# A dilated-attention layer with gated MLP: five step times of the attention plan moved, so that its small matmuls stand in other places

## The chip, the cores and the metric

One core of one Trainium2 chip. The metric is device microseconds (us) of one execution; the kernel before takes 1303.2 us, the median of three runs (1301.95 to 1303.62). Engines are named as the profile names them: PE is TensorE (PEld its weight loads), DVE is VectorE, ACT is ScalarE, POOL is GpSimd, SP is the queue that issues the DMAs.

## What is computed

One layer of a decoder trunk on 1024 tokens of width 1024. The mixer is a dilated sliding-window attention with 3 groups (dilations 1, 4, 16) of 8 heads of 64; the groups are merged by their softmax denominators. After it comes a gated MLP of 2 x 2816 channels with a short causal convolution. Cut to what matters:

```
h = rms_norm(x, mixer_norm)
proj = (h @ w_in).reshape(B, S, 3 groups, 3, 8 heads, 64)
for g, (window, dilation) in enumerate(((128, 1), (512, 4), (2048, 16))):
    q = rms_norm(proj[:, :, g, 0], q_gain[g]) * 64 ** -0.5
    k = rms_norm(proj[:, :, g, 1], k_gain[g])
    o, lse = dilated_window_attention(q, k, proj[:, :, g, 2], window, dilation)
o = sum over groups of softmax(lse) * o
x = x + o @ w_out
x = x + conv_ffn(rms_norm(x, ffn_norm))
```

All is in float32. A product of two float32 matrices is made of three matmuls on numbers split into a high and a low part.

## The kernel before

The attention runs as 48 blocks: 6 units (a group and half of its heads: group 2, then 1, then 0, two units each) of 8 blocks of 128 tokens. Units are counted from 0 here, blocks from 0 to 47; units 4 and 5 are the last group, and their blocks also merge the three groups. Of a block, PE makes the projection of q and k (lines 207 to 209, matmuls of 512 columns, 24 of them), the projection of v (lines 216 to 218, 256 columns, 24 of them) and small work: four transposes of the normed q and k (line 265, tile `tr`), the scores (lines 294, 298), the transposes of the softmax weights of heads 0 and 1, then of heads 2 and 3 (line 331, tile `pt`), and the second products, weights times v, for the same two pairs of heads (lines 349 and 351, tile `u`, 128 and 64 columns). A block with a previous block of keys (22 of the 48) has twice the weights: 4 transposes and 8 second products for a pair of heads, the others 2 and 4.

Nothing is scheduled by a planner. Every step of a block is put into one list with a time, counted in steps of one projection slice; a block has 8. The list is sorted by time, equal times in the order in which they were added, and PE, ACT, DVE and POOL each run their instructions in just that order. For block i:

```
e = 8 * i + 8
at(8 * i + k, b.project, k)                      # k = 0..7
at(8 * i + T["vs"] * k + T["v"], b.project_v, k) # 2.6 + 0.85 k
at(e + T[name] + late, step, *args)              # all other steps
```

So a block's small steps lie between the projections of the two blocks after it. The steps in question, by their name in the table `T` (line 35):

- `w0`, `w1` (weights_T): the transposes of the weights on PE. `ws0`, `ws1` (weights_split): each result is copied to its high part by ACT (line 337) and the low part is made by DVE (line 338, tile `pT`).
- `a0`, `a1` (attend): the second products on PE. A first matmul of a pair needs the high part, the second (line 351) the low part.
- `scale` (line 229, DVE, tile `qn`): the normed q and k of the next block. `hT` (line 265, PE) transposes them, `hs` splits them on ACT and DVE (lines 276 to 282), and the scores follow. `scale` needs the reciprocal root `rs` from POOL (line 80).
- `mw` (units 4 and 5): line 370 and 372 on DVE, line 373 (an exponential) on ACT, line 375 and on on POOL.
- `load_w`: the split of the next unit's projection weights, the high part on ACT (line 188), the low part on DVE or POOL (line 189).
- Behind the last blocks the second phase begins: line 628 and 629 split the output weights, lines 584 to 586 are the output projection, line 588 adds it to x, and `norm2` (line 593 on ACT, line 595 on DVE) norms the sum.

Times of other steps that lie near: `scale` of the next block at e + 10.5, its `hT` at e + 12.2, `mw` at e + 10.0, `load_w` at e + 8.7, 9.45 and 10.6 (start of units 2 and 4) or e + 8.7, 9.6 and 10.8 (units 1, 3 and 5), `norm2` of the first output rows at e + 9.8 of block 47.

Of the kernel before, what the change touches and what calls it, by code (L numbers as in the profile page):

```python
# [32 lines left out]


T = dict(v=2.6, vs=0.85, w=3.1, norm=-0.2, val=0.6, kept=3.2, scale=2.5, hT=4.2, hs=4.45, sc=6.45,
         sm=6.5, w0=8.3, ws0=9.35, w1=10.0, ws1=11.95, mw=10.0, a0=12.2, a1=13.3, mo=12.2,
         fin=14.4, t0=4, so0=3.2, so1=3.3, so2=5.1, so3=5.2, to0=-3.43, to=-3.6, n2=3.0, n2s=5.8,
         xf=-9.8, xs=-5.0, xt=-3.5, wp=1, bd=0.5, bh=0)

# [1067 lines left out]
```

## Time and profile before

| | |
|---|---|
| median of 3 runs | 1303.2 us (1301.95 to 1303.62) |
| the profiled execution | 1301.99 us |
| its span, first to last instruction | 1300.0 us |
| PE busy | 1274.2 us, 98% of the span |
| DVE, ACT, POOL busy | 69%, 47%, 37% |
| granted clock of PE | 0.999 |

The attention's blocks fill the span from about 11 to 582 us, some 11.9 us each; the output projection and the MLP follow. A timeline row gives an instruction's start from the span's start, its duration, engine, line, output and inputs, and in brackets the idle time of its engine before it and who ended that. Rows of matmuls overlap: PE takes the next one before the last has drained. So what a matmul costs is read from start to start, not from its duration.

### The profile page before, as it was taken

The numbers are of one execution on the slowest core, as the hardware profiler recorded it, in microseconds if no ns is written. First come the engines' busy times: TensorE is split into PE (matmuls) and PEld (weight loads), VectorE is DVE, ScalarE is ACT, GpSimd is POOL, SyncE is SP. The second block draws the span as 40 slices with busy tenths as digits, with TensorE's granted clock in tenths as the row PEclk, the third lists the DMA queues.
The fourth block names the chain that finished last, engine by engine and source line by source line (L and its number), as shares of the span: only waits on it lengthen the run. The fifth ranks groups of instructions, "written<-read, shape, count | busy, mean of one in ns | idle before, by whom it ended". The sixth has DMA issues, their size and how long they took to land.

```text
span 1300.0 us, 19219 instructions
## 1 busy us (share of the span) xinstructions
PE 1274.2 (98%) x6911; PEld 1071.0 (82%) x6911; DVE 896.2 (69%) x1542; ACT 617.1 (47%) x1284; POOL 486.7 (37%) x596
## 2 busy tenths in 40 slices
PE   7999999999999999999998999999999999999998
PEld 6888888888888888887886788888888887888887
DVE  5665555555555665557876988888888888876664
ACT  5555454444464454345644454544544545444441
POOL 4333443332454555535523544444444442000000
PEclk9999999999999999999999999999999999999999
DMA  7112112111131221023711333233233229963341
GB/s 263 38 54 79 38 38 60 47 48 52 46 109 51 62 63 37 27 70 132 235 35 43 120 122 122 81 114 105 66 122 122 81 81 326 367 212 97 97 143 63
DMA packets 111614, 132.16 MB, mean 102 GB/s; under 512 B 6126, under 2 KB 80030, under 8 KB 111518
## 3 DMA queue, kind: packets, MB, share of 16 engines
q1 hardware_dynamic: 111518, 130.93, 31.5%
q8 instruction: 55, 0.90, 0.3%
q14 instruction: 41, 0.34, 0.1%
HBM read 95.91 MB, written 35.00 MB: 101 GB/s over the span
## 4 chain that ended last, share of the span: by engine, by line
PE 43%; DVE 4%; ACT 2%; issue 1%; DMA 1%; POOL 0%; SPq 0%; DVEq 0%; POOLq 0%; ACTq 0%
PE y L902 15%; PE ua L718 15%; PE uc L718 8%; PE ub L718 4%; DVE c L763 2%; ACT c L761 1%; DMA x<-in_x 1%; DMA graw<-gde 0%; DVE bt L629 0%; DVE sz L691 0%; DVE c L774 0%; DVE xn L595 0%; DMA wB<-in_ffn_w_down 0%; DVE sy L687 0%; POOL b L629 0%
## 5 line engine op out<-in xcount | busy, mean ns | idle before, releaser
L902 PE MATMUL y<-wd,g 128*128 128x512 f32 x924 | 210.4, 389 | 0.2
L902 PEld LDWEIGHTS y<-wd,g 128*128 128x128 f32 x924 | 173.4, 188 | 36.9 <-DVE wd L629 0.6
L207 PE MATMUL qk<-w,hh 128*128 128x512 f32 x384 | 157.5, 410 | 0.1
L208 PE MATMUL qk<-w,hh 128*128 128x512 f32 x384 | 152.8, 398 | 0.3 <-DVE w L189 0.3
L209 PE MATMUL qk<-w,hl 128*128 128x512 f32 x320 | 126.1, 394 | 0.0
L79 POOL TENSOR_SCALAR ms<-ss 128x8 f32<-128x8 f32 (+1 forms) x64 | 12.8, 201 | 296.6 <-DVE ss L225 254.0
L763 DVE SCALAR_TENSOR_TENSOR c<-uu,cw,c 128x1023 f32<-128x1023 f32 (+1 forms) x44 | 97.0, 2205 | 37.1 <-ACT c L761 36.3
L216 PE MATMUL vp<-w,hh 128*128 128x256 f32 x384 | 122.0, 318 | 0.4 <-DVE v L237 0.2
L217 PE MATMUL vp<-w,hh 128*128 128x256 f32 x384 | 107.9, 281 | 0.0
L549 POOL TENSOR_TENSOR wyl<-sy,wyh 128x1024 fp32r<-128x1024 f32 x21 | 56.9, 2708 | 109.3 <-issue 55.3
L80 POOL TENSOR_TENSOR rs<-ms,half 128x8 f32<-128x8 f32 (+1 forms) x64 | 89.0, 1391 | 5.3
L218 PE MATMUL vp<-w,hl 128*128 128x256 f32 x320 | 90.0, 281 | 0.0
L323 ACT ACTIVATE sm<-sm,ust 128x128 f32<-128x128 f32 (+1 forms) x128 | 53.3, 418 | 77.0 <-DVE ust L320 74.5
L216 PEld LDWEIGHTS vp<-w,hh 128*128 128x128 f32 x384 | 72.8, 189 | 15.2 <-DVE v L237 2.4
L225 DVE TENSOR_REDUCE ss<-qn 128x8 f32<-128x512 f32 x48 | 32.9, 685 | 75.6 <-ACT qn L223 75.6
L276 ACT ACTIVATE qT<-tr,gains 128x256 fp32r<-128x256 f32 x48 | 22.7, 474 | 122.0 <-PE tr L265 122.0
L217 PEld LDWEIGHTS vp<-w,hh 128*128 128x128 f32 x384 | 72.8, 190 | 9.1
L279 DVE SCALAR_TENSOR_TENSOR qT<-tr,gains,qT 128x256 fp32r<-128x256 f32 x48 | 23.1, 482 | 81.4 <-ACT kT L278 81.4
L208 PEld LDWEIGHTS qk<-w,hh 128*128 128x128 f32 x384 | 73.1, 190 | 1.5 <-DVE w L189 1.0
L207 PEld LDWEIGHTS qk<-w,hh 128*128 128x128 f32 x384 | 73.0, 190 | 0.7 <-ACT hh L116 0.5
L320 DVE CUSTOM_DVE_ANT_0 sm<-s,mask 128x128 f32<-128x128 f32 (+1 forms) x192 | 56.0, 347 | 24.0 <-PE s L298 18.5
L209 PEld LDWEIGHTS qk<-w,hl 128*128 128x128 f32 x320 | 60.5, 189 | 14.6 <-DVE hl L117 0.2
(193 smaller groups left out, 3395.7 us busy)
## 6 DMA issues: line engine op xcount, KB each, us to landing
uraw<-in_ffn_w_up SPq DMA_DIRECT2D x44, 512.0 KB
raw<-in_attn_w_in SPq DMA_DIRECT2D x48, 384.0 KB
wB<-in_ffn_w_down SPq DMA_DIRECT2D x44, 256.0 KB
graw<-gds SPq DMA_DIRECT2D x44, 256.0 KB
gdo<-c SPq DMA_DIRECT2D x11, 512.0 KB
gds<-gbc SPq DMA_DIRECT2D x11, 512.0 KB
graw<-gdo SPq DMA_DIRECT2D x22, 256.0 KB
ud<-ust SPq DMA_DIRECT2D x32, 132.0 KB
```

Of the source, the lines that this page charges most:

```text
L80: nc.gpsimd.tensor_tensor(r[:, :n], t[:, :n], half[:, :n], op=ALU.pow)
L207: nc.tensor.matmul(self.qk, a, w[:, 0, :512], start=k == 0, stop=False)
L208: nc.tensor.matmul(self.qk, a, w[:, 1, :512], start=False, stop=False)
L209: nc.tensor.matmul(self.qk, b, w[:, 0, :512], start=False, stop=k == KT - 1)
L216: nc.tensor.matmul(self.vp, a, w[:, 0, 512:], start=k == 0, stop=False)
L217: nc.tensor.matmul(self.vp, a, w[:, 1, 512:], start=False, stop=False)
L218: nc.tensor.matmul(self.vp, b, w[:, 0, 512:], start=False, stop=k == KT - 1)
L320: nc.vector.tensor_tensor_reduce(out=sm[:, h, lo:], in0=src[h], in1=m, op0=ALU.add, op1=ALU.min, scale=-1.0, scalar=3e38, accum_out=st[:, ...
L549: eng.tensor_sub(l, raw, h.bitcast(F32))
L718: nc.tensor.matmul(acc[:, lo:hi], w[z][:, s + k], a[y][:, j, k, lo:hi], start=begin and lo == 0 and k == 0 and n == 0, stop=k == 3 and n == 2,
L763: nc.vector.scalar_tensor_tensor(c[:, k:], u[:, :S - k], cw[:, 2 - k, j:j + 1], c[:, k:], op0=ALU.mult, op1=ALU.add)
L902: nc.tensor.matmul(y, gs[:, z, ts], ws[:, w], start=f and n == 0, stop=k == NK - 1 and n == 2, skip_group_check=True)
```

## The change

Five numbers of the table are changed: `w0` from 8.3 to 9.0, `ws0` from 9.35 to 9.9, `w1` from 10.0 to 9.05, `ws1` from 11.95 to 10.5, and `a1` from 13.3 to 12.25. Each holds for all 48 blocks. No instruction is added or dropped.

```diff
-         sm=6.5, w0=8.3, ws0=9.35, w1=10.0, ws1=11.95, mw=10.0, a0=12.2, a1=13.3, mo=12.2,
+         sm=6.5, w0=9.0, ws0=9.9, w1=9.05, ws1=10.5, mw=10.0, a0=12.2, a1=12.25, mo=12.2,
```

On PE, the transposes of the weights in a block without previous keys; `vp` and `qk` are the projections of later blocks. Before:

```order
2066 L331 MATMUL pt<-ident,sm 128x128 x2
2067 L216 MATMUL vp<-w,hh 128x256
2068 L217 MATMUL vp<-w,hh 128x256
2069 L218 MATMUL vp<-w,hl 128x256
2070 L207 MATMUL qk<-w,hh 128x512
2071 L208 MATMUL qk<-w,hh 128x512
2072 L209 MATMUL qk<-w,hl 128x512
2073 L331 MATMUL pt<-ident,sm 128x128 x2
```

The same place after:

```order
2066 L216 MATMUL vp<-w,hh 128x256
2067 L217 MATMUL vp<-w,hh 128x256
2068 L218 MATMUL vp<-w,hl 128x256
2069 L331 MATMUL pt<-ident,sm 128x128 x2
2070 L207 MATMUL qk<-w,hh 128x512
2071 L208 MATMUL qk<-w,hh 128x512
2072 L209 MATMUL qk<-w,hl 128x512
2073 L331 MATMUL pt<-ident,sm 128x128 x2
```

The first pair moves behind three matmuls of 256 columns; the second pair keeps its place, and a slice of the q and k projection (whose time, 9.0, equals the new `w0` and comes before 9.05) still stands between the two.

On PE, the second products in such a block; `tr` are the next block's transposes of q and k, behind `a0`:

```order
 L351 MATMUL u<-v,pT 128x64
 L265 MATMUL tr<-ident,qn 128x128 x4
+L349 MATMUL u<-v,pT 128x128
+L351 MATMUL u<-v,pT 128x64
+L349 MATMUL u<-v,pT 128x128
+L351 MATMUL u<-v,pT 128x64
 L216 MATMUL vp<-w,hh 128x256
 L217 MATMUL vp<-w,hh 128x256
```

The second products of heads 2 and 3 now follow `tr` at once; before they stood three slices of projection later.

On DVE, a block of units 4 and 5 with previous keys; `pT` is the low part of `ws1`, `qn` the next block's `scale`:

```order
 L370 TENSOR_REDUCE nm<-mt 128x4
 L372 TENSOR_TENSOR e<-nm,mt 128x12
-L229 TENSOR_TENSOR qn<-qk,rs 128x512
-L338 TENSOR_TENSOR pT<-pt,pT 128x512
+L338 TENSOR_TENSOR pT<-pt,pT 128x512
+L229 TENSOR_TENSOR qn<-qk,rs 128x512
 L386 RECIPROCAL rz<-z 128x4
 L279 SCALAR_TENSOR_TENSOR qT<-tr,gains,qT 128x256
```

`ws1` and `scale` change places, since both stand at 10.5 and the earlier block's step was added first. It is so in every block.

On DVE, block 47, where the second phase has begun; `x_7030` and `x_7033` are the same tile, the first output rows, in before and after. Before:

```order
893 L588 TENSOR_TENSOR x_7030<-x_7030,y 128x512
894 L338 TENSOR_TENSOR pT<-pt,pT 128x512
895 L595 SCALAR_TENSOR_TENSOR xn<-x_7030,rs,gbc 128x1024
896 L370 TENSOR_REDUCE nm<-mt 128x4
897 L372 TENSOR_TENSOR e<-nm,mt 128x12
898 L588 TENSOR_TENSOR x_7152<-x_7152,y 128x512
899 L338 TENSOR_TENSOR pT<-pt,pT 128x512
```

The same place after:

```order
859 L588 TENSOR_TENSOR x_7033<-x_7033,y 128x512
860 L595 SCALAR_TENSOR_TENSOR xn<-x_7033,rs,gbc 128x1024
861 L338 TENSOR_TENSOR pT<-pt,pT 128x512
862 L370 TENSOR_REDUCE nm<-mt 128x4
863 L372 TENSOR_TENSOR e<-nm,mt 128x12
864 L588 TENSOR_TENSOR x_7154<-x_7154,y 128x512
865 L338 TENSOR_TENSOR pT<-pt,pT 128x512
```

`ws0` of block 47 (9.9) moves behind `norm2` (9.8), here on DVE and in the same way on ACT. At the start of a unit `ws0` likewise moves behind one more `load_w` (9.45 or 9.6) on ACT and DVE, and `ws1` moves ahead of the one at 10.6 or 10.8.

## Rows read from the trace of the kernel before

**Rows 1.** The page's first part: busy time, share, instructions of PE.

```profile
PE 1274.2 (98%) x6911; PEld 1071.0 (82%) x6911; DVE 896.2 (69%) x1542; ACT 617.1 (47%) x1284; POOL 486.7 (37%) x596
```

**Rows 2.** Waits of PE and of DVE: who for whom, total us, times, longest us.

```profile
PE tr L265 <- DVE qn L229: 2.9, 5, 0.9
...
DVE qn L229 <- POOL rs L80: 42.0, 41, 1.5
```

**Rows 3.** Timeline of PE, `a1` of a block with previous keys, and behind it.

```profile
306.67 0.22 PE L349 MATMUL u<-v,pT 128*128 128x128 f32 x1
...
307.48 0.37 PE L216 MATMUL vp<-w,hh 128*128 128x256 f32 x1
307.68 0.29 PE L217 MATMUL vp<-w,hh 128*128 128x256 f32 x1
307.81 0.28 PE L218 MATMUL vp<-w,hx 128*128 128x256 f32 x1
```

**Rows 4.** Timeline of PE, `a1` of block 47, which stands between transposes.

```profile
604.66 0.31 PE L349 MATMUL u<-v,pT 128*128 128x128 f32 x1
...
605.55 0.33 PE L605 MATMUL xT<-ident,xn 128*128 128x128 f32 x1
```

**Rows 5.** Timeline, block 34 (unit 4): `mw`, `scale`, `ws1`, `tr`.

```profile
434.53 0.17 DVE L372 TENSOR_TENSOR e<-nm,mt 128x12 f32<-128x12 f32 x1
434.62 0.68 DVE L229 TENSOR_TENSOR qn<-qk,rs 128x512 f32<-128x512 f32 x1
...
435.45 0.69 DVE L338 TENSOR_TENSOR pT<-pt,pT 128x512 fp32r<-128x512 f32 x1 [0.15 <-ACT pT L337]
...
436.26 0.33 PE L265 MATMUL tr<-ident,qn 128*128 128x128 f32 x1
```

**Rows 6.** Timeline, block 43 (unit 5): `ws1` on ACT, `tr`.

```profile
545.95 0.57 ACT L337 CAST pT<-pt 128x512 fp32r<-128x512 f32 x1
...
548.42 0.33 PE L265 MATMUL tr<-ident,qn 128*128 128x128 f32 x1
```

**Rows 7.** Timeline, block 38, where unit 5's weights are split.

```profile
484.69 1.83 POOL L189 TENSOR_TENSOR w<-raw,w 128x768 fp32r<-128x768 f32 x1
...
484.82 1.72 DVE L372 TENSOR_TENSOR e<-nm,mt 128x12 f32<-128x12 f32 x1
...
486.47 0.68 DVE L229 TENSOR_TENSOR qn<-qk,rs 128x512 f32<-128x512 f32 x1
...
487.21 0.33 PE L265 MATMUL tr<-ident,qn 128*128 128x128 f32 x1 [0.49 <-DVE qn L229]
```

**Rows 8.** Timeline, block 30, where unit 4's weights are split.

```profile
387.38 0.68 DVE L229 TENSOR_TENSOR qn<-qk,rs 128x512 f32<-128x512 f32 x1
...
387.98 0.41 DVE L338 TENSOR_TENSOR pT<-pt,pT 128x256 fp32r<-128x256 f32 x1
...
388.11 0.33 PE L265 MATMUL tr<-ident,qn 128*128 128x128 f32 x1 [0.92 <-DVE qn L229]
```

**Rows 9.** Timeline, block 47: `ws0`, `norm2`, `a0`, `ws1`.

```profile
597.09 0.56 ACT L337 CAST pT<-pt 128x512 fp32r<-128x512 f32 x1
...
597.55 1.06 ACT L593 ACTIVATE xn<-x 128x1024 f32<-128x1024 f32 x1
...
599.65 1.29 DVE L595 SCALAR_TENSOR_TENSOR xn<-x,rs,gbc 128x1024 f32<-128x1024 f32 x1 [1.28 <-POOL rs L80]
...
600.26 0.22 PE L349 MATMUL u<-v,pT 128*128 128x128 f32 x1
...
601.97 0.69 DVE L338 TENSOR_TENSOR pT<-pt,pT 128x512 fp32r<-128x512 f32 x1 [0.16 <-ACT pT L337]
```

**Rows 10.** Timeline, `a1` of blocks 22 and 46: first matmuls.

```profile
294.24 0.22 PE L349 MATMUL u<-v,pT 128*128 128x128 f32 x1
...
294.55 0.30 PE L351 MATMUL u<-v,pT 128*128 128x64 f32 x1
...
589.50 0.30 PE L351 MATMUL u<-v,pT 128*128 128x64 f32 x1 [0.40 <-DVE pT L338]
```

## The prediction

> **What bounds the kernel now.** The page's first part comes first: PE is busy for 98% of the span [rows 1], so the end moves only with what PE itself costs or waits. Then the waits of PE and of DVE [rows 2]. In the attention PE waits above all for one thing, the transposes `tr` of the next block for DVE's `scale` (2.9 us in 5 waits), and DVE's `scale` itself mostly waits for POOL's `rs` (42.0 us in 41 waits). So DVE usually stands idle in front of `scale`, and whatever is put there is free as long as it fits; where it doesn't fit, PE waits at `tr`. Last the timeline, for two questions: what a group of small matmuls costs apart and joined [rows 3, 4], and how close each kind of block is to making `tr` wait [rows 5 to 9].
>
> **The joined groups on PE.** `a1` alone, 8 second products, runs from 306.67 to 307.48, 0.81 us, and the first big matmul behind it holds the next one off for 0.20 us where the one after takes 0.13 [rows 3]: 0.81 + 0.07 = 0.88 us for the group. `a1` of block 47 already stands directly behind transposes: 604.66 to 605.55, 0.89 us [rows 4]. So the slow restart behind a group is real, but a group that stands alone gets the same back at its head, where its first weights were loaded during a long matmul. Joining 47 groups `a1` to `tr` is priced at 0. The bounds: 0.07 x 47 = 3.3 us gained, if the restart were saved and the fast head kept; 0.08 x 47 = 3.8 us lost (0.89 against 0.81), if the head were lost and the restart stayed. The rows nearest to the new place are rows 4, hence 0. `w0` only moves behind three projection matmuls and `w1` does not move among PE's instructions at all: 0, since neither pair is joined to the other. That `w0` comes later is covered by ACT, which works on the softmax and the next block's squares until then; if that cover were gone, `a0` would wait for `ws0`.
>
> **`ws1` ahead of `scale`, ordinary blocks.** In units 0 to 3 `w1` is done early and DVE idles before `scale` until POOL is done [rows 2]; `ws1` fits there: 0. In units 4 and 5 it does not come early, because ACT first makes the exponential of `mw`, which waits for DVE's L372. A typical block of unit 5: ACT ends `ws1` at 545.95 + 0.57 = 546.52; DVE then needs 0.62 us for `ws1` (0.69 long, the next one starts 0.07 before its recorded end, as L229 does after L372 [rows 7]) and 0.68 for `scale`, and `tr` follows 0.06 later: 547.9, where PE comes to `tr` at 548.42 [rows 6]. Half a microsecond is left; eight blocks are of this kind (33, 36, 39, 41 to 45), and I price them at 0.
>
> In blocks 34 and 35 a split of the next unit's weights stands before `ws0`, and there it doesn't fit. Block 34: L372 ends at 434.70 and `ws1` starts on DVE at 435.45, 0.75 us behind it, with an idle DVE released by ACT; `scale` was made before that, at 434.62 [rows 5]. Now `scale` follows at 435.45 + 0.62 = 436.07, ends at 436.75, and `tr` starts at 436.81 instead of 436.26: +0.55. Two such blocks: **+1.1**. What then waits on PE is all that stands behind `tr`; nothing gives it back, since the next scores and their softmax start from PE again.
>
> **Starts of units.** Block 38 (unit 5's weights): L372, 12 elements, took 1.72 us instead of 0.17, and ended at 486.54 together with POOL's low part of a weight slice, 484.69 + 1.83 = 486.52 [rows 5, 7]. `scale` came right behind it and `tr` already waited 0.49 us. Now the 0.75 us to `ws1` and `ws1` itself come between: `ws1` at 487.29, `scale` at 487.91 to 488.59, `tr` at 488.65 instead of 487.21: **+1.44**. The moved weight split does not help, since POOL starts its part only after `rs`. On this the Trainium skill, "SBUF — State Buffer", section "Who interferes with whom", says that VectorE with two inputs in SBUF and GpSimd share a port pair as an exclusive lock, the later one blocking until the first is through; the row fits it. By that rule L372 stays locked out to the same 486.5 in the new order too; were the 1.72 us only an accident of the old order, this term would be about 0.3 and the whole sum 1.1 lower.
>
> Blocks 14 and 30 (units 2 and 4): DVE goes into `scale` with no idle time and PE already waits 0.92 us for it [rows 8]. `ws1` now stands in front, 0.41 - 0.07 = 0.34 us each: **+0.7**. Blocks 6 and 22 (units 1 and 3) have `scale` waiting for POOL: 0. There `a1` had waited for its low part, with 0.31 us between its first two matmuls [rows 10]; `ws1` is now done before `tr`, so some 0.3 us go in each of the two: **-0.6**.
>
> **The end of the attention.** Block 47's `ws0` moves behind `norm2` on ACT and DVE. On ACT L593 then starts where `ws0` did, 597.55 - 597.09 = 0.46 us earlier, so that L595 runs on DVE from 599.19 to 600.48. `ws0` follows on DVE from 600.41 to 601.10, where before it had been done long before `a0` [rows 9]. PE comes to `a0` at 600.26 and now waits for the low part until 601.16. `ws1` started at 601.97, 1.03 us after L595's end at 600.94, with `mw` and an L588 between; they now follow `ws0`: 601.10 + 1.03 = 602.13, done at 602.82. Before, `a1` stood 3.6 us behind `a0`'s end [rows 4] and did not care; now it is next, from 600.26 + 0.81 = 601.07 [rows 3, 9], and its first low part is wanted at some 601.2 and comes at 602.88: **+1.7** for both waits. Block 46: one wait of 0.40 us goes [rows 10], one `ws1` of 0.69 us comes ahead of `scale`; between -0.4 and +0.7, and I take **+0.2**.
>
> **Sum.** 1.1 + 1.44 + 0.7 - 0.6 + 1.7 + 0.2 = +4.5 us. Against the profiled execution's own 1301.99 us (span 1300.0) this gives 1306.5; the median of the runs shown is 1.2 above that execution, so **1307.7 us** is forecast for the median.
>
> **Rivals.**
> (a) The two dear places turn out cheap: in block 38 L372 slips in before POOL's long instruction, and in block 47 L595 is ready before `ws0` wants DVE. For it: both terms are built from single places and on an order never seen. Against it: L595 waits for POOL, which waits for L593, and DVE takes its instructions in order. It decides where L595 ends before 600.2. Then 4.5 - 1.1 - 1.7 = +1.7: 1304.9, no change.
> (b) The restart is saved outright: 4.5 - 3.3 = +1.2: 1304.4, no change. Against it stand rows 4.
> (c) Faster: in the longer groups the second products run at the pace of a group's head. Rows 3 give 0.20 us for a pair in the run of 8 (0.81 / 4); the 0.07 us of a restart saved on each of the 140 pairs of `a1` would be 9.8 us, and 4.5 - 9.8 = -5.3: 1297.9. It decides from the first pair on that follows `tr`. Against it: in rows 4 the joined group keeps the old pace. The Trainium skill, "TensorE: Matmul & The Clock Gate", section "Back-to-back issue gap", states about 81 ns for a sustained matmul of 128 columns with its weight load; by that the 280 matmuls of `a1` would save some 8 us, an estimate from that page, but no group here runs so fast.
> (d) Slower still: the half microsecond left in the eight blocks of units 4 and 5 is used up, because `ws1` comes over 0.5 us later than in rows 6. At another 0.5 us in seven of them, +3.5: 1311.2.
>
> **How the numbers follow.** Forecast 0.62 (own range 1306.3 to 1309.2), (a) 0.22, (b) 0.04, (c) 0.05, (d) 0.07. About 0.2%, 2.6 us, is what a measurement of this kernel tells from no change: faster below 1300.6, slower above 1305.8. The forecast and (d) are slower: 0.69; (a) and (b) no change: 0.26; (c) faster: 0.05. The range 1304.3 to 1310.8 holds the forecast and nearly all of (a) and (b), and leaves out (c) and most of (d).
>
> **What will show it.** `a1` behind `tr` at 0.22 us for two matmuls, 0.89 us for 8, and no shorter group in sum. PE's wait of `tr` for `scale` up from 2.9 to some 6 us, with waits in blocks 34 and 35 that were not there, and one of about 2 us in block 38. Two new waits of `u` for `pT`, 0.8 and 0.9 us, in block 47; the waits of `u` in blocks 6 and 22 gone. The forecast is wrong if `a1` runs at a quicker pace behind `tr`, if `tr` starts in block 38 as early as before, or if PE does not wait at the end of the attention.

## The result

The changed kernel takes 1309.18 us in the median of four runs (1308.85 to 1310.8), the kernel before 1302.61 beside it: a ratio of 1.0055, 95% interval 1.0043 to 1.0067. It is slower by 6.6 us, where 4.5 were forecast; the forecast, 1307.7, had the sign and its range held the time. Its sum did not come out term by term, though: two terms were too small, one too large.

The page of the kernel after: busy time, share of the span (1307.2 us) and instructions of PE, and PE's granted clock in 40 slices. PE is busy 5.3 us longer with the same 6911 instructions [rows 1], and one slice, the one at 588 to 621 us, is no longer at 9 (before, all 40 are).

```profile
PE 1279.5 (98%) x6911; PEld 1077.2 (82%) x6911; DVE 896.7 (69%) x1542; ACT 613.2 (47%) x1284; POOL 494.1 (38%) x596
...
PEclk9999999999999999998999999999999999999999
```

The waits of PE, after (who for whom, total us, times, longest): `tr` waits 5.6 us for `scale` in place of 2.9, but in 12 places in place of 5 [rows 2] (the view puts the waits in blocks 34 and 35 down to `rz`, DVE's next instruction, and they come on top), and `u` for the low parts of the weights 2.0 us.

```profile
PE tr L265 <- DVE qn L229: 5.6, 12, 1.4
PE u L351 <- DVE pT L338: 2.0, 4, 0.6
```

To see where the time goes, the starts of each block's first `tr`, of the scores and of the output projection were taken from both traces and their difference followed from mark to mark. A step of this difference is what the change costs between two marks. As in the prediction, a step "in block n" is one at the `tr` that follows block n's `w0` and `ws1`.

| place | forecast | measured, us |
|---|---|---|
| joining `a1` to `tr`, 47 blocks | 0 | 0 (each 0.04 at most) |
| blocks 2, 3, 10, 11, 18, 26 | 0 | +2.45 (0.38 to 0.42 each) |
| blocks 34, 35 | +1.1 | +1.02 |
| block 38 | +1.44 | +0.19 |
| blocks 14, 30 | +0.7 | +0.88 |
| blocks 6, 22 | -0.6 | -0.46 |
| blocks 46, 47, first output rows | +1.9 | +3.8 |
| start of the program | 0 | -0.5 |
| smaller steps | 0 | -0.2 |
| sum | +4.5 | +7.2 |

The sum is that of the two profiled executions, whose spans are 1307.2 and 1300.0 us; the medians lie 6.6 us apart. The start is the arrival of the first tokens, which differs from run to run (-0.5 to +0.3 in the kernels below). Behind the first output rows both traces run in step to the end: nothing is given back.

**The six new waits.** Timeline of block 10, start, duration, engine, line, tile. The kernel before:

```profile
150.62 1.64 POOL L80 TENSOR_TENSOR rs<-ms,half 128x8 f32<-128x8 f32 x1
150.74 0.96 DVE L189 TENSOR_TENSOR w<-raw,w 128x768 fp32r<-128x768 f32 x1 [0.16 <-ACT w L188]
...
152.29 0.69 DVE L229 TENSOR_TENSOR qn<-qk,rs 128x512 f32<-128x512 f32 x1 [0.26 <-POOL rs L80]
...
153.48 0.66 PE L265 MATMUL tr<-ident,qn 128*128 128x128 f32 x4
```

The kernel after:

```profile
150.57 0.96 DVE L189 TENSOR_TENSOR w<-raw,w 128x768 fp32r<-128x768 f32 x1
150.63 2.39 POOL L80 TENSOR_TENSOR rs<-ms,half 128x8 f32<-128x8 f32 x1
...
153.06 0.69 DVE L229 TENSOR_TENSOR qn<-qk,rs 128x512 f32<-128x512 f32 x1 [0.87 <-POOL rs L80]
...
153.90 0.52 PE L265 MATMUL tr<-ident,qn 128*128 128x128 f32 x3 [0.26 <-DVE qn L229]
```

`w0` now stands behind the last `vp` matmuls in place of ahead of them, so v is ready earlier, ACT's copy of it comes earlier, and the weight split behind that copy too: its high part (L188) starts at 149.69, before at 149.87. DVE's low part (L189) then starts 0.06 us ahead of POOL's `rs` (L80), not 0.12 behind it. That is enough: `rs`, eight numbers per partition, takes 2.39 us in place of 1.64, `scale` comes 0.77 later, the cover of some 0.4 us is gone, and PE waits. A wait in brackets falls some 0.17 us short of the step that it makes: 0.26 beside 0.42 here, 0.33 beside 0.51 in block 34.

**Joined groups.** Timeline of PE, after, a block with previous keys, the 8 second products behind `tr`: 306.52 to 307.42, 0.90 us.

```profile
306.52 0.31 PE L349 MATMUL u<-v,pT 128*128 128x128 f32 x1
...
307.42 0.37 PE L216 MATMUL vp<-w,hh 128*128 128x256 f32 x1
```

The whole group of `a0`, `tr` and `a1` holds the projection up for 1.30 us with 4 and 4 second products, and for 2.20 us with 8 and 8; before, its two pieces took 0.85 + 0.45 and 1.30 + 0.90. A sum, to 10 ns.

**Blocks 34, 38 and 30.** After, block 34: `ws1` stands ahead of `scale`, which ends at 438.77, and `tr` starts 0.51 later than before (2.66 us of difference, against 2.14 in the block ahead) [rows 5].

```profile
436.56 0.17 DVE L372 TENSOR_TENSOR e<-nm,mt 128x12 f32<-128x12 f32 x1
...
437.48 0.69 DVE L338 TENSOR_TENSOR pT<-pt,pT 128x512 fp32r<-128x512 f32 x1 [0.75 <-ACT pT L337]
438.09 0.68 DVE L229 TENSOR_TENSOR qn<-qk,rs 128x512 f32<-128x512 f32 x1
...
438.92 0.63 PE L265 MATMUL tr<-ident,qn 128*128 128x128 f32 x4 [0.33 <-DVE rz L386]
```

After, block 38. Here too L80 is the slow one (2.40 us, 0.06 behind DVE's L189); POOL therefore begins its own long split only at 488.61, and L372 has slipped in before, at 488.19, in 0.17 us and not 1.72 [rows 7].

```profile
486.18 0.96 DVE L189 TENSOR_TENSOR w<-raw,w 128x768 fp32r<-128x768 f32 x1
486.24 2.40 POOL L80 TENSOR_TENSOR rs<-ms,half 128x8 f32<-128x8 f32 x1
...
488.19 0.17 DVE L372 TENSOR_TENSOR e<-nm,mt 128x12 f32<-128x12 f32 x1
...
488.61 1.82 POOL L189 TENSOR_TENSOR w<-raw,w 128x768 fp32r<-128x768 f32 x1
...
490.55 0.63 PE L265 MATMUL tr<-ident,qn 128*128 128x128 f32 x4 [0.67 <-DVE qn L229]
```

After, block 30 [rows 8]: the wait is now shared between `a0` (0.60 us, for `ws0`, which stands behind one more weight split) and `tr` (0.50), and the step is 0.44 us.

```profile
389.25 0.30 PE L351 MATMUL u<-v,pT 128*128 128x64 f32 x1 [0.60 <-DVE pT L338]
...
390.27 0.63 PE L265 MATMUL tr<-ident,qn 128*128 128x128 f32 x4 [0.50 <-DVE qn L229]
```

**The end of the attention.** After, block 47: `a0` waits 0.64 us for its low part and `a1` 0.40.

```profile
603.66 0.68 DVE L338 TENSOR_TENSOR pT<-pt,pT 128x512 fp32r<-128x512 f32 x1
...
604.39 0.30 PE L351 MATMUL u<-v,pT 128*128 128x64 f32 x1 [0.64 <-DVE pT L338]
...
605.37 0.69 DVE L338 TENSOR_TENSOR pT<-pt,pT 128x512 fp32r<-128x512 f32 x1 [0.16 <-ACT pT L337]
...
606.12 0.30 PE L351 MATMUL u<-v,pT 128*128 128x64 f32 x1 [0.40 <-DVE pT L338]
```

Busy time of the engines in stretches of the same place, after; the number behind POOL is PE's granted clock. It falls to the lower of its two levels (1.2 in place of 2.4 GHz) for some 3 us behind these waits. In the kernel before all stretches from 600 to 613 us are at 1.00.

```profile
604.00:607.00 3.00, 2.18 (x16) 1.93 (x17) 1.96 (x6) 0.69 (x2) 1.31 (x5) 1.00 0.01 3
607.00:609.00 2.00, 2.00 (x10) 1.71 (x9) 0.47 (x1) 0.59 (x1) 1.43 (x3) 0.53 0.15 9
609.00:611.00 2.00, 2.00 (x7) 1.61 (x6) 0.21 (x1) 0.00 (x0) 0.00 (x0) 0.61 0.91 329
```

### The profile page after: what moved, and what is told of

Read it like the earlier page. It is cut to its first block, busy times and chain, and to the rows that moved or that the text cites. A ratio compares the mean times of both kernels' runs of the same rounds, so it can differ in the third digit from the quotient of the medians.

```text
span 1307.2 us, 19311 instructions
## 1 busy us (share of the span) xinstructions
PE 1279.5 (98%) x6911; PEld 1077.2 (82%) x6911; DVE 896.7 (69%) x1542; ACT 613.2 (47%) x1284; POOL 494.1 (38%) x596
## 4 chain that ended last, share of the span: by engine, by line
PE 44%; DVE 4%; ACT 2%; issue 1%; DMA 1%; POOL 1%; SPq 0%; DVEq 0%; POOLq 0%; ACTq 0%
PE ua L718 16%; PE y L902 15%; PE uc L718 8%; PE ub L718 4%; DVE c L763 1%; ACT c L761 1%; DMA graw<-gde 0%; DVE bt L629 0%; DMA wB<-in_ffn_w_down 0%; DVE xn L595 0%; POOL b L629 0%; DVE sz L691 0%; DVE x L588 0%; POOL wzl L549 0%; POOL wxl L549 0%
## 5 line engine op out<-in xcount | busy, mean ns | idle before, releaser
L207 PE MATMUL qk<-w,hh 128*128 128x512 f32 x384 | 160.8, 419 | 0.0
L208 PE MATMUL qk<-w,hh 128*128 128x512 f32 x384 | 152.7, 398 | 0.4 <-DVE w L189 0.3
L216 PE MATMUL vp<-w,hh 128*128 128x256 f32 x384 | 114.2, 297 | 0.9 <-DVE v L237 0.9
L217 PE MATMUL vp<-w,hh 128*128 128x256 f32 x384 | 108.1, 281 | 0.0
L80 POOL TENSOR_TENSOR rs<-ms,half 128x8 f32<-128x8 f32 (+1 forms) x64 | 97.4, 1522 | 5.3
L549 POOL TENSOR_TENSOR wzl<-sz,wzh 128x1024 fp32r<-128x1024 f32 x21 | 55.5, 2643 | 44.5 <-ACT wzh L548 29.5
```

The costliest lines, as they stand in the source:

```text
L80: nc.gpsimd.tensor_tensor(r[:, :n], t[:, :n], half[:, :n], op=ALU.pow)
L207: nc.tensor.matmul(self.qk, a, w[:, 0, :512], start=k == 0, stop=False)
L208: nc.tensor.matmul(self.qk, a, w[:, 1, :512], start=False, stop=False)
L216: nc.tensor.matmul(self.vp, a, w[:, 0, 512:], start=k == 0, stop=False)
L217: nc.tensor.matmul(self.vp, a, w[:, 1, 512:], start=False, stop=False)
L549: eng.tensor_sub(l, raw, h.bitcast(F32))
```

## The experiments

Unless said otherwise, a kernel here is the changed kernel with the edit shown, of long lines only what changes; steps are again differences to the kernel before, from mark to mark.

### The second products put back

```diff
-         a1=12.25
+         a1=13.3
```

> Undoes one part: the second products (a1) stand 1.05 later in the table again, as a group of their own in every block; all else is as in the changed kernel. Theory: joining the groups cost and saved nothing (0.852 + 0.448 us apart, 1.30 us joined), so the steps from block to block stay as in the changed kernel to within 0.02 us; only block 47 gets cheaper, since a1 no longer waits there for its low part: 0.4 us less, and 1.8 us more less if the low granted clock at the start of the output projection comes from that wait. Time 1306.5 to 1308.8 us, against 1309.2 of the changed kernel. Blocks 6 and 22 stay without a wait of u for pT. Rival: the longer groups have a price or a gain of their own on each of 47 blocks (0.07 to 0.08 us each): the time would move by over 3 us, to 1306 or to 1312.5, spread evenly over the blocks.

Measured: 1307.71 us, ratio to before 1.004 (1.0027 to 1.0052). From `tr` to `tr`, every step up to block 45 is that of the changed kernel to within 0.05 us, and there is no wait of `u` in blocks 6 and 22. Five of the six waits are there. In place of block 3's, 0.30 us come ahead of the scores behind block 2's `tr`; in block 3 L189 starts 0.05 us behind L80, and L80 takes 1.65 us. So joining is worth nothing, in either direction, and the rival of 3 us falls. What changed is the end: +2.1 us in place of +3.8. The wait itself did not go: `a0` of block 47 now waits 1.11 us for its low part, as much as `a0` and `a1` together did (1.04). The clock behind it stayed up:

```profile
604.00:607.00 3.00, 1.89 (x15) 1.55 (x14) 2.81 (x6) 0.69 (x2) 0.42 (x2) 1.00 0.00 0
607.00:609.00 2.00, 2.00 (x12) 1.69 (x11) 1.34 (x3) 0.59 (x1) 1.39 (x4) 1.00 0.24 48
```

The 1.7 us between the two kernels are not yet the price of the low clock at 607 to 611: `a1` stands elsewhere too, and this kernel lost 0.8 us ahead of the second output row, with its clock at 0.50 from 594 to 598 us. The run with the first two groups joined, below, shows the price with both waits in place.

### `ws1` behind `scale` again

```diff
-         ws1=10.5
+         ws1=10.55
```

> Undoes one part: the softmax of the first half (ws1) stands behind scale again (10.55 in place of 10.5), all else as in the changed kernel. Theory: the steps that the prediction put on ws1 ahead of scale go: blocks 14 and 30 0.44 us each, blocks 34 and 35 0.51 each, block 38 some 0.2; sum -2.1, so 1307.1 us. The six new waits of tr in blocks 2, 3, 10, 11, 18 and 26 (0.4 us each) stay, since scale waits there for POOL's rs and not for ws1. Block 38: L372 no longer depends on where scale stands, so it slips in before POOL's low part again and tr waits under 0.5 us. Rival: the order of ws1 and scale is what makes the six waits: then they go as well, sum -4.5, 1304.7 us.

Measured: 1306.01 us, ratio 1.0029 (1.0018 to 1.0039). Blocks 14 and 30 step by 0.02 and 0.05 (block 31 by another 0.32), 34 and 35 by 0.01, block 38 by -0.64; five of the six waits are there, 0.39 to 0.42 each. The sixth, in block 3, is gone, and there L189 starts 0.02 us behind L80. So these terms belong to `ws1` ahead of `scale`, and the six waits do not. The end of the attention came out 0.7 us cheaper as well, which was not expected: `a0` and `a1` of block 47 wait 1.11 and 0.40 us, more than in the changed kernel, but the granted clock is at 1.00 from 598 us on (it was down earlier, from 590 to 597 us).

### The next unit's weights one step later

```diff
-         wp=1
+         wp=2
```

> Leaves the order of the changed kernel but moves the preparation of the next unit's weights (the table's wp, 2 in place of 1) one step later in each block, so that ACT's split L188 and DVE's L189 come behind ws0. Theory: the six new waits of tr (blocks 2, 3, 10, 11, 18, 26) exist because DVE's L189 starts 0.06 us ahead of POOL's L80, which then takes 2.39 us instead of 1.64; with L189 behind, L80 takes about 1.64 us again and the six waits go: -2.4 us, 1306.8 us. Rival: L80 is slow there because of what stands before it on POOL, or tr waits because w0 and ws0 come later: L80 stays at 2.4 us or tr still waits by 0.4 us in these blocks, and the time stays within 0.5 us of 1309.2.

Measured: 1307.92 us, ratio 1.0042 (1.0029 to 1.0054); its runs lie between 1305.16 (mean granted clock 1.000) and 1309.64 (0.995), so the median says little, and the steps decide: all six waits are gone (0.00 to 0.01 each), 34 and 35 stay (0.44 each), and so does the end (+3.9 with the low clock). Block 10 of this kernel:

```profile
150.38 1.64 POOL L80 TENSOR_TENSOR rs<-ms,half 128x8 f32<-128x8 f32 x1
...
150.59 0.96 DVE L189 TENSOR_TENSOR w<-raw,w 128x768 fp32r<-128x768 f32 x1
...
152.05 0.69 DVE L229 TENSOR_TENSOR qn<-qk,rs 128x512 f32<-128x512 f32 x1 [0.16 <-POOL rs L80]
```

L80 starts first and takes 1.64 us again, with `w0` and `ws0` where the change put them.

### `w0` put back

```diff
-         w0=9.0
+         w0=8.3
```

> Undoes one part: the first transposes of the weights (w0) stand at 8.3 again, the low part (ws0) stays at 9.9, all else as in the changed kernel. Theory: PE reaches the last of vp later by w0's own time (about 0.2 us against the rest of the block), so ACT's copy of v and its split L188 come 0.18 us later, DVE's L189 starts behind POOL's L80, and the six waits of tr go: -2.4 us, 1306.8 us. The end of the attention stays at +3.8 against the kernel before. Rival: the six waits come from ws0 at 9.9 or ws1 ahead of scale: they stay and the time is 1309.2 us within 0.5.

Measured: 1311.43 us, ratio 1.0071 (1.0058 to 1.0085). The mechanism came as expected, the time did not. The six waits are gone, so it is `w0` that makes them. But in block 38 L80 is now quick as well, POOL's split starts at 485.57, and L372 is locked out again:

```profile
485.57 1.84 POOL L189 TENSOR_TENSOR w<-raw,w 128x768 fp32r<-128x768 f32 x1
...
486.05 1.38 DVE L372 TENSOR_TENSOR e<-nm,mt 128x12 f32<-128x12 f32 x1
...
488.19 0.69 DVE L338 TENSOR_TENSOR pT<-pt,pT 128x512 fp32r<-128x512 f32 x1 [0.75 <-ACT pT L337]
488.80 0.68 DVE L229 TENSOR_TENSOR qn<-qk,rs 128x512 f32<-128x512 f32 x1
```

`tr` steps by +1.45 in block 38: the 1.44 of the prediction, in the order that it described. What the prediction had not seen is the 3.1 us that follow. PE waited 1.94 us at that `tr`, and the clock fell (stretches of 2 us, the clock behind POOL):

```profile
487.00:489.00 2.00, 0.59 (x6) 0.48 (x5) 1.25 (x3) 1.42 (x3) 1.50 (x6) 1.00 0.00 0
...
491.00:493.00 2.00, 2.00 (x10) 2.00 (x10) 1.47 (x3) 0.45 (x2) 1.71 (x3) 0.50 0.00 0
493.00:495.00 2.00, 2.00 (x8) 1.71 (x8) 0.42 (x1) 0.00 (x0) 0.73 (x1) 0.50 0.00 0
```

### The end put back

```diff
-         ws0=9.9, a1=12.25
+         ws0=9.35, a1=13.3
```

> Undoes two parts, a1 (13.3) and ws0 (9.35); w0, w1 and ws1 stay as in the changed kernel. Theory: the end of the attention costs 3.8 us more than before because a0 and a1 of block 47 wait for their low parts and the granted clock is 0.50 for some 4 us around them. With ws0 ahead of norm2 and a1 late neither waits; what is left there is a clock fall around 593 us behind the wait of tr in block 47 (in the run with a1 alone put back the clock was 0.50 from 594 to 598). So y(2) stands 0 to 1.4 us behind its place before, instead of +3.3, and the time is 1306 to 1308. The six waits of tr stay. Rival: the six waits come from ws0 at 9.9: then they go too, 1303.5 to 1305.5.

Measured: 1305.99 us, ratio 1.0029 (1.0017 to 1.004). Between the second and the third row of the output projection the step is 0.00 (after: +3.32), and the end costs +0.7 in all; five of the six waits stay at 0.38 to 0.44, so they do not come from `ws0` (block 3 is as in the run with `a1` put back). Of the 3.8 us, 3.1 belong to `ws0` behind `norm2` and `a1` behind `tr`.

### The first two groups really joined

```diff
-         w0=9.0
+         w0=9.04
```

> Goes one step further than the change: w0 at 9.04, so that it stands directly ahead of w1 with no projection matmul between, and a block really has three groups. Theory: a group of small matmuls costs the sum of its parts (0.22 us for two transposes, 0.44 for four, apart or joined), so every ordinary block's step stays as in the changed kernel to within 0.02 us and the time is 1309.2 within 0.7. Rival: each group has a price of its own, at least 0.07 us: 47 groups fewer would give 3.3 us back, 1305.9 us.

Measured: 1311.95 us, ratio 1.007 (1.0056 to 1.0083), the runs from 1309.27 to 1314.01. The profiled execution, 1309.27, is that of the changed kernel within 0.1 us, and its ordinary blocks step by the same; one stretch behind block 30, with the clock at 0.50 from 392 to 394 us, costs 1.5 us, and the first output rows give 1.6 back. A joined pair holds the projection up for 0.436 us in place of 0.219 + 0.221, and for 0.873 in place of 0.442 + 0.440: 46 groups fewer are worth 0.3 us at most, a tenth of what the rival needs. The four other executions are slower at a lower mean granted clock, 0.993 to 0.996 where the profiled one had 0.998, so falls of the clock are the likely cause; it is not shown, since no trace of them is at hand.

This trace also prices the low clock at the end of the attention. `a0` and `a1` of block 47 wait 0.62 and 0.40 us, as in the changed kernel, but the clock stays at 1.00:

```profile
609.00:611.00 2.00, 2.00 (x12) 1.67 (x11) 0.69 (x1) 0.59 (x1) 1.15 (x2) 1.00 0.31 83
611.00:613.00 2.00, 2.00 (x15) 1.75 (x14) 0.94 (x2) 0.50 (x2) 0.00 (x0) 1.00 0.81 310
```

From the start of the second output row to that of the fourth it loses 2.2 us on the kernel before, the changed kernel 3.85: the waits take 2.2 us there and the low clock 1.6. The wait at block 47's `tr` is the same too, 1.44 us, and here no fall follows it.

### The kernel before, with other places for the weights

From the kernel before, nothing of the change:

```diff
-  (3.9, *((8.7, 9.45, 10.6, 12.6) if u % 2 == 0 else (5.4, 8.7, 9.6, 10.8)))[kt - SP]
+  (3.9, *((8.64, 10.55, 10.6, 12.6) if u % 2 == 0 else (5.4, 9.4, 10.55, 10.8)))[kt - SP]
```

> The kernel before with nothing of the change, but other places for the preparation of the late weight slices: 8.64, 10.55, 10.6, 12.6 in units of even number (before 8.7, 9.45, 10.6, 12.6) and 5.4, 9.4, 10.55, 10.8 in those of odd number (before 5.4, 8.7, 9.6, 10.8), so that the weight split that stands ahead of scale in the first block of a unit comes behind it. Theory: the waits of tr in blocks 6, 14, 22, 30 and 38 of the kernel before (2.9 us together) and the waits of u in blocks 6 and 22 (0.3 each) go: -2 to -3.5 us against the kernel before, 1298.5 to 1300. Rival: the weights come too late for the first slices of the next unit, and the waits turn up at the projection instead: 1302 or slower.

Measured: 1301.39 us, ratio 0.9994 (0.9985 to 1.0003), no difference that the runs can tell. `tr` comes earlier by 0.59, 0.62, 0.56, 0.99 and 0.66 us in the five places, as the theory said; but what was won in blocks 14, 30 and 38 is given back behind them. In block 14:

```profile
197.81 1.82 POOL L189 TENSOR_TENSOR w<-raw,w 128x768 fp32r<-128x768 f32 x1 [0.36 <-ACT w L188]
198.08 2.36 DVE L189 TENSOR_TENSOR w<-raw,w 128x768 fp32r<-128x768 f32 x1
...
200.49 0.50 PE L208 MATMUL qk<-w,hh 128*128 128x512 f32 x1 [1.03 <-DVE w L189]
```

POOL began its split 0.27 us before DVE, DVE's took 2.36 us in place of 0.96, and the projection waited 1.03 us for it.

### Waits of known length

From the kernel before. Here blocks are counted by the `scale` that is repeated, which is one more than in the table above.

```diff
         def scale(self):
-            nc.vector.tensor_tensor(self.qn, ...
+            for _ in range(1 + {12: 1, 20: 2, 28: 3, 44: 4}.get(8 * self.u + self.c, 0)):
+                nc.vector.tensor_tensor(self.qn, ...
```

> The kernel before, with scale done again (same instruction, same result) 1, 2, 3 and 4 more times in blocks 12, 20, 28 and 44, and once in all others, to measure what a wait of PE costs by its length. Each further scale is 0.62 to 0.68 us of DVE ahead of tr, of which 0.5 us is covered: waits of tr of about 0.1, 0.75, 1.4 and 2.0 us. Theory: a short wait costs itself and nothing more; a long one is followed by a stretch at a granted clock of 0.50 and costs some 3 us more, as in block 38 of the kernel with w0 put back (wait 1.94 us, and 3.1 us lost by the next scores). So about +0.1, +0.75, +1.4 (or +4.5) and +5, in all 7 to 11 us. Rival: the low clock there had another cause, and a wait costs only its own length: +4.3 us in all, clock 1.00 throughout.

Measured, one run: steps of +0.29, +0.35, +1.09 and +1.87 us, +3.5 at the end of the attention, and a clock of 1.00 throughout; 1306.09 us against 1302.22. The rival held: these waits cost their length alone. Behind the longest, in block 44, with PE idle for 1.70 us of this stretch, the clock stayed up:

```profile
550.00:552.00 2.00, 0.30 (x3) 0.19 (x3) 1.93 (x4) 0.00 (x0) 0.00 (x0) 1.00 0.00 0
```

A second run of the kind:

```diff
-            for _ in range(1 + {12: 1, 20: 2, 28: 3, 44: 4}.get(8 * self.u + self.c, 0)):
+            for _ in range(1 + {20: 5, 30: 1, 38: 2, 46: 1}.get(8 * self.u + self.c, 0)):
```

> The kernel before, with scale done again 5 more times in block 20, once in block 30, 2 times in block 38 and once in block 46. From e8_stalls each further scale adds 0.7 us to the wait of tr once the cover of 0.5 us is gone: 2.6 us in block 20, 1.6 in block 30, 1.9 in block 38, 0.2 in block 46. Theory: what brings the clock down is the length of the wait, with the limit between 1.87 us (block 44, clock 1.00) and 1.94 us (block 38 with w0 put back, clock 0.50): a fall behind block 20, perhaps one in block 38, none behind blocks 30 and 46; in all +6 us and some 3 us for each fall. Rival: the place counts, that is what PE did shortly before and after the wait: falls behind blocks 30 and 38, where PE also waits for weights or low parts, and not necessarily behind block 20.

Measured, one run: block 20 steps by 2.53 us, PE waits 2.38 there, the clock falls towards the end of the wait, and the next scores come another 1.23 late.

```profile
258.00:260.00 2.00, 0.89 (x5) 0.89 (x5) 1.62 (x3) 0.00 (x0) 0.00 (x0) 0.62 0.00 0
260.00:262.00 2.00, 2.00 (x9) 1.73 (x8) 0.38 (x1) 1.30 (x3) 0.00 (x0) 0.53 0.00 0
```

The other three waits missed their places: by the count of the edit, the waiting starts of units are blocks 31 and 39, and in 30, 38 and 46 the cover held all but 0.4 us. So the rival, that the place counts, was not tested. Yet the clock fell at 593 us too and cost 1.2 us, with no wait added near it. Length alone doesn't settle it either: after 1.70 us in block 44 there was no fall, after 1.44 us at block 47's `tr` of the changed kernel there was one (0.50 from 594 to 596 us), and after the same 1.44 us with the first two groups joined there was none. What decides stays open.

### The change, with `ws1`, the weights and block 47 put elsewhere

```diff
-         ws1=10.5
+         ws1=10.55
-         wp=1
+         wp=2
+            if b is blocks[-1] and name in ("ws0", "a1"):
+                late = -.55 if name == "ws0" else 1.05
```

> Keeps the three groups of the change in all blocks but the last (w0 9.0, w1 9.05, a1 12.25) and takes away everything that was found to cost: ws1 behind scale (10.55), the next unit's weights behind ws0 (wp 2), and in block 47 alone ws0 and a1 at their old places. Theory: the joins are worth nothing, and the cost is the sum of the neighbours' waits, so the time comes back to that of the kernel before: -0.5 for the waits of u that are gone in blocks 6 and 22, -0.6 in block 38, -0.1 to +0.4 around block 47 (a clock fall at 593 us may stay): 1301 to 1302.5 us. Rival: the joined groups cost something of their own that the other runs hid; then it stays above 1304.5.

Measured: 1300.75 us, ratio 0.9989 (0.998 to 0.9998). The small matmuls stay where the change put them, but for those of block 47, and the cost is gone, so all of it lay in the neighbours' order and in block 47. `tr` of block 47 waits 1.03 us, as with `ws1` alone put back, but the clock that fell there stays at 1.00 here. The kernel is a shade under before: 0.3 from an early start, 0.6 from block 38, and 0.2 from each of blocks 6 and 22, less 0.3 in block 31.

### From the kernel before: weight splits moved, one of them to DVE

From the kernel before:

```diff
-  (nc.vector if kt in (0, 2, 4, 5, 7) else nc.gpsimd).tensor_sub(w[:, 1], ...
+  (nc.vector if kt in (0, 2, 4, 5, 7) or kt == 6 and u in (2, 4) else nc.gpsimd).tensor_sub(w[:, 1], ...
-  (3.9, *((8.7, 9.45, 10.6, 12.6) if u % 2 == 0 else (5.4, 8.7, 9.6, 10.8)))[kt - SP]
+  (3.9, *((8.64, 10.55, 10.6, 12.6) if u % 2 == 0 else
+          (5.4, 9.4, 10.55, 10.8) if u < 5 else (5.4, 8.7, 9.6, 10.8)))[kt - SP]
```

> The kernel before without any joined group, with the weight splits of a unit's first blocks moved out of the way: the places of the run e7_loads for units 1 to 4, those of before for unit 5, and in units 2 and 4 slice 6 split by DVE in place of POOL, directly behind slice 5, so that POOL's long instruction no longer runs beside DVE's. Theory: the waits of tr in blocks 6, 14, 22 and 30 go (-0.73, -0.62, -0.75, -0.99, as in e7_loads up to that point) and nothing is given back behind them, since DVE's slice 5 took 2.36 us in e7_loads only beside POOL's: -3.1 us, 1299.1 us, the one kernel here that beats before. Rival: two splits in a row, 1.9 us of DVE, hold up the queries' and keys' low parts that the scores need, and 0.5 to 1 us comes back in each of blocks 14 and 30: 1300.1 to 1301.1 us.

Measured: 1299.22 us, ratio 0.9978 (0.997 to 0.9987), 3.1 us faster. At the end of the attention it is 3.0 us ahead (0.5 of that from the start). In block 14 the two splits on DVE take 1.82 us together, no longer beside POOL's, and the projection doesn't wait for them:

```profile
196.69 0.69 DVE L229 TENSOR_TENSOR qn<-qk,rs 128x512 f32<-128x512 f32 x1 [0.75 <-POOL rs L80]
197.30 1.82 DVE L189 TENSOR_TENSOR w<-raw,w 128x768 fp32r<-128x768 f32 x2
...
197.44 0.66 PE L265 MATMUL tr<-ident,qn 128*128 128x128 f32 x4 [0.44 <-DVE qn L229]
```

Block 30 gave 0.6 of its 0.99 back, as the rival said it might; block 14 gave back nothing. Another 0.8 us is lost in the MLP, where PE waits 1.05 us in place of 0.27 for a sum on DVE (L738 of the kernel before); the first run of waits lost 0.6 at the same place. Why DVE is late there is open.

Last, these weights (slice 5 at 10.57) in the changed kernel with `ws1`, `wp` and block 47 put elsewhere, as above:

> The two best runs together: the three groups as in e9_mended, and the weight splits as in e10_best (slice 5 at 10.57, so that it comes behind ws1). Theory: the gains sit at different places and add up: e9_mended's 0.6 us in block 38 and 0.5 us at the end of unit 5, and e10_best's 3.0 us at the starts of units 1 to 4 (less what both take from the waits of u in blocks 6 and 22, 0.3 us): 3.5 us under the kernel before in the attention, 1298.7 us. Rival: behind ws1 the two splits of slices 5 and 6 come 0.7 us later than in e10_best, so that the projection waits for them at the starts of units 2 and 4: no better than e10_best, 1299 to 1300.5 us.

Measured: 1299.51 us, ratio 0.9978 (0.9968 to 0.9987), the same as with the weights alone. Blocks 14 and 30 gain (-0.59, -0.94) and give nothing back, so the rival's mechanism is not there. Two other things are: blocks 6 and 22 gain 0.2 each in place of 0.7, and the granted clock is 0.50 from 586 to 592 us, which takes some 0.5 us.

```profile
588.00:590.00 2.00, 2.00 (x15) 1.53 (x13) 2.00 (x3) 0.59 (x1) 2.00 (x2) 0.50 0.03 8
```

## Why the prediction was right, and where not

- **The joins, 0.** Right, and for its reason: a group behind `tr` takes 0.90 us where rows 4 had 0.89, and with the groups apart again nothing moved. Rivals (b) and (c) fall. The 81 ns for a matmul that the Trainium skill states, "TensorE: Matmul & The Clock Gate", section "Back-to-back issue gap", show in no group here: 8 take 0.90 us, 112 ns each.
- **`w0` at 0, "covered by ACT".** Here the sum failed. The step asked who waits for what comes *later*, and that answer was right. It did not ask what comes *earlier*: the matmuls that `w0` left behind it, the copy of v that they release, the weight split behind that. Six splits started 0.18 us sooner, ahead of `rs` and no longer behind it: +2.45 us that no term held. That `w0` is the cause is shown by putting it back, that the order of L189 and L80 is, by moving the weights alone. "`ws1` fits there: 0" was right for the same blocks.
- **Blocks 34 and 35, 14 and 30, 6 and 22.** Right in place and size: 1.02 for 1.1, 0.88 for 0.7, -0.46 for -0.6. The first two go when `ws1` stands behind `scale`. The eight other blocks of units 4 and 5 cost nothing, so rival (d) falls.
- **Block 38, 1.44.** The chain was right and its premise wrong, that L372 stays locked out: POOL's split started after L372, since L80 was late. This is rival (a)'s first half. With L80 quick, the run with `w0` put back shows the 1.45.
- **The end, 1.7 + 0.2.** The two waits were there, and smaller than forecast: 0.64 and 0.40 in place of 0.8 and 0.9. The step that failed is the price of a wait: it was put at its length, and the clock that fell behind it cost another 1.6 us, by the run with the first two groups joined, which has these waits without the fall.
- **The total.** It came near by luck, because a term too large by 1.25 stood against 2.45 and 1.9 that were missing. The sign to look for, `tr` waiting "some 6 us", came true as well (5.6), and in other blocks than those named: a total that fits does not show that its parts do.

On the shared port pair the rows say more than before. The Trainium skill, "SBUF — State Buffer", section "Who interferes with whom", has an instruction of VectorE with two inputs in SBUF and one of GpSimd that reads SBUF contend; section "SBUF: two separate sides" says of their lock that whichever starts first has the pair for the whole instruction. Block 10 agrees where DVE is first: L80 is held up, 0.75 us. It doesn't where POOL is first: L189 starts 0.12 us behind L80, while that still has 1.5 us to run, and takes its plain 0.96. A long split on POOL does hold DVE up (2.36 in place of 0.96). What happened in block 10 holds in every block where the two overlap, in six traces (before, after and the first four runs): `rs` took 2.32 to 2.46 us where L189 started ahead of it, by 0.00 to 0.14 us, and 1.64 or 1.65 where it started 0.02 us or more behind. In the changed kernel that made `rs` slow in eleven blocks where it had been quick; in five of them, 19, 27, 34, 35 and 38, the cover or another wait hid nearly all of it.

## What to carry to other kernels

When a step is moved later in an engine's order, list also what moves earlier because of it, along its consumers to the next engine, and look there for pairs of DVE and POOL instructions that start within some 0.1 us of each other: their order decides. A wait of TensorE of about 1 us, or two shorter ones close together, may cost more than its length in one execution and not in the next, so read the granted clock of the stretch behind it, in more than one trace, before pricing the wait. And put steps of long weight preparation behind, not ahead of, the short instruction that TensorE waits for next; here that, with one split moved from POOL to DVE, was worth 3 us, where regrouping the matmuls was worth nothing.

## What was not expected of the hardware

- An instruction of POOL on 128x8 elements takes 1.64 or 2.39 us, by whether DVE's 128x768 subtraction begins 0.12 us behind it or 0.06 ahead of it.
- Around waits of 1.94 and 2.38 us TensorE's granted clock was down to 0.50, its lower level of 1.2 GHz, for some 7 and some 3 us, and the next scores came 3.1 and 1.2 us later than the wait alone makes them; behind one of 1.70 us it stayed at 1.00.
- The same waits went both ways. Behind 1.44 us at block 47's `tr` the clock fell in the changed kernel and stayed up with the first two groups joined; behind 1.03 us there it fell with `ws1` put back and stayed up with the weights and block 47 moved as well; behind 0.64 and 0.40 us it fell in the changed kernel, behind 0.62 and 0.40 with the groups joined it did not. It differs between executions of one kernel too: with `ws1` put back, three had a mean granted clock of 1.000 and took 1305.26 to 1305.50 us, five had 0.996 or 0.997 and took 1305.95 to 1306.95. What decides is not shown.
- A low clock ahead of a wait can cost nothing: in the changed kernel it was 0.50 from 594 to 596 us too, and the next output rows stood no further behind (3.65 us at block 47's `tr`, 3.28 at the second row). With `a1` put back it was 0.50 from 594 to 598 us, and the second row stood 0.4 us further behind (3.86, 4.30).
